# Where the persistent tiles and the second branch's tiles of a projection-bound decoder block lie in a partition

## The chip, the cores and the metric

One core of one Trainium2 chip runs the whole kernel. The metric is the device time of one execution in microseconds. An execution that the hardware profiler took gives the profile; the median of three further runs is the time that counts.

## What is computed

One hybrid decoder block on x of 512 tokens by 1024 channels, float32. A normalisation, then one wide input projection feeds two branches, whose gated outputs are merged, projected and normalised:

```python
hN = _rmsnorm(x, norm_g[l])
p = _split_in(hN @ w_in[l])            # 8992 columns, all from the same hN
mh = _mlstm(q, k, v, i_gate, f_gate)   # 4 heads x 256, q and k after a conv of width 4
ya = sigmoid(p["m_o"]) * headnorm(mh) * silu(p["m_z"])
yn = _nsa(...)                         # 8 heads x 64: compressed, selected and window attention
yb = yn * silu(p["n_z"])
merged = sigmoid(p["g_a"]) * (ya @ w_branch_a[l]) + sigmoid(p["g_b"]) * (yb @ w_branch_b[l])
x = x + merged @ w_out[l]
return _rmsnorm(x, final_norm_g)
```

With 512 tokens the selection takes every block, so the selected and the window branch are both full causal attention.

## The kernel before, in words

Every large product is done in three passes: each float32 operand is split into a high part, rounded to the matmul's input type float32r, and a low part, the residue (`split`, line 125: ACT copies the high part, DVE subtracts). hTh and hTl are the two parts of the normalised input, transposed: 128 partitions, 8 slices k of 512 tokens. Weights come in tiles of 8 slices by 128 columns (or 4 by 256): a DMA into wr, then the split into wh and wl, three buffers of each (`weights`, line 136).

A projection (`cols`, line 206) makes 128 output columns for all 512 tokens in one PSUM bank, 24 matmuls: for each of the 8 slices high weights by hTh, high weights by hTl, low weights by hTh (`passes`, line 195). The weight slice is the stationary operand, the 512 tokens are streamed:

```python
pe.matmul(ps, a, c, start=k == 0, stop=False)       # line 198: wh by hTh
pe.matmul(ps, a, d, start=False, stop=False)        # line 200: wh by hTl
pe.matmul(ps, b, c, start=False, stop=k == nk - 1)  # line 202: wl by hTh
```

The profile names a matmul by the streamed tile first, then the stationary one: pp<-hTh,wh. Each matmul also loads its stationary operand, 128 columns, which the profile lists as PEld. `passes` is a generator: the `Stream` (line 160) holds a queue of projections in a fixed order, and the other parts of the kernel take a few matmuls out of it at a time (`stream.step`, `tick`), to fill TensorE while ACT and DVE work.

The order of the work: normalisation and transposes, with a first product for small columns at line 356 (hTh and hTl are the stationary operand there); the first projections; the attention of 16 units, four projection matmuls between its steps (`tick`, line 810); then for the first branch the convolution's projections and the values, per head (`conv`, line 888, and `values`, line 909); the four heads with six matmuls between steps; then the branch stage (line 1050): for each of 8 column blocks two gate projections (`gate_ab`, streams hTh and hTl, as far as they were not done before), 24 matmuls that stream yah and yal (the first branch's output), 12 that stream ybh and ybl (the second's); last the output projection (line 1084, through `mm3`, line 152).

In the values and in the output projection the roles are turned: the weights are streamed, 256 columns wide, and 128 tokens of hTh or hTl, of meh or mel, are the stationary operand.

Where tiles lie. Each `tile` call takes the next bytes of its pool in every partition, its size rounded up to 32 bytes. The pool pers (line 91) holds, in this order, cst (5152 bytes), hTh and hTl (16384 each), mhalf, prm, cpos, rotR, gates, li, lf, ghl (2048 bytes), sel, Fc, cs and em. Without the three large ones, those behind cst sum to 32 + 352 + 128 + 512 + 384 + 64 + 64 + 32 + 64 + 64 + 64 = 1760 bytes. The pool wp follows with the nine weight buffers of 4096 bytes. Behind these lie, in the first phases, the tiles of the attention, later yah and yal, the tiles of the first branch's heads, and meh and mel. The pool ybp (line 444) is on the right side, against the upper end: ybh, ybl (8192 bytes each) and two more of 2048. gate and the compression's tiles lie below it. In the program of before the first bytes are:

| tile | first byte | modulo 512 |
|---|---|---|
| hTh, hTl | 21664, 38048 | 160 |
| wh (three buffers) | 70528, 74624, 78720 | 384 |
| wl (three buffers) | 82816, 86912, 91008 | 384 |
| yah, yal | 95104, 111488 | 384 |
| ybh, ybl | 208864, 217056 | 480 |

A slice k is 2048 bytes from the next in hTh, hTl, yah, yal, ybh and ybl, and 512 bytes (1024 where the tile is 256 columns wide) in wh and wl.

Of the kernel before, what the change touches and what calls it, by code (L numbers as in the profile page):

```python
# [12 lines left out]
F32R = mybir.dt.float32r  # L13
# [5 lines left out]
T = 512  # L19
D = 1024  # L20
NT = T // 128
ND = D // 128
# [41 lines left out]
def build(  # L64
# [26 lines left out]
    pers = ctx.enter_context(tc.tile_pool(name="pers", bufs=1))  # L91
# [13 lines left out]

    cst = pers.tile([128, CEND], F32, name="cst")
    ident = cst[:, CI : CI + 128]

    hTh = pers.tile([128, ND, T], F32R, name="hTh")
    hTl = pers.tile([128, ND, T], F32R, name="hTl")  # L110

    mhalf = pers.tile([128, 4], F32, name="mhalf")
    pool.memset(mhalf, -0.5)
# [113 lines left out]
    gates = pers.tile([128, NT, 24], F32, name="gates")  # L227
    li = pers.tile([128, NT, 4], F32, name="li")
    lf = pers.tile([128, NT, 4], F32, name="lf")
    ghl = pers.tile([128, T], F32R, name="ghl")  # L230
    sel = pers.tile([128, 4], F32R, name="sel")
    Fc = pers.tile([128, NT, 4], F32, name="Fc")
    cs = pers.tile([128, NT, 4], F32, name="cs")
    em = pers.tile([128, NT, 4], F32, name="em")

    nsa = tc.tile_pool(name="nsa", bufs=1)
    np_ = nsa.__enter__()
# [9 lines left out]
    with tc.tile_pool(name="ph0", bufs=2, side="right") as p0, tc.tile_pool(  # L247
        name="small", bufs=1, side="right"
# [194 lines left out]

    ybp = ctx.enter_context(tc.tile_pool(name="ybp", bufs=1, side="right"))
    ybh = ybp.tile([128, 4, T], F32R, name="ybh")
    ybl = ybp.tile([128, 4, T], F32R, name="ybl")
    halves = {}

    def gate_ab(base, j, pl):
# [677 lines left out]
```

## Time and profile before

| | |
|---|---|
| median of 3 runs | 649.25 us (648.68 to 649.99) |
| the profiled execution | 650.03 us |
| its span, first to last instruction | 648.2 us |
| granted TensorE clock, mean | 0.998 |

The span is what the profile covers; the 1.8 us more of the profiled execution lie around it. PE is TensorE's matmuls and PEld its loads of the stationary operand, DVE is VectorE, ACT is ScalarE, POOL is GpSimd. Ends of matmuls are modelled and matmuls overlap, so the pace of TensorE is read from the distance of starts.

### The profile page before, as it was taken

The page shows a single profiled execution, that of the slowest core. Times are in us where ns is not written, and L with a number is a line of the kernel's source. Part 1 is how long each engine was busy: PE and PEld are TensorE (multiplying, and loading weights), DVE is VectorE, ACT ScalarE, POOL GpSimd, SP SyncE. Part 2 cuts the span into 40 slices and gives each one's busy share as a digit, 9 for nine tenths or more (in the row PEclk, how much of TensorE's full clock was granted, in tenths as well). Part 3 has the DMA queues.
Part 4 walks back from the last instruction along what each step waited for, and adds up shares of the span by engine and source line. Part 5 has one row for each costly group of instructions (what it writes and reads, how often), then busy time and mean ns, then how long its engine had stood idle before and what let it go on. Part 6 is the DMA issues. An engine that isn't in the chain of part 4 may idle for free.

```text
span 648.2 us, 9274 instructions
## 1 busy us (share of the span) xinstructions
PE 632.3 (98%) x3470; PEld 538.4 (83%) x3470; DVE 412.2 (64%) x878; ACT 302.8 (47%) x604; POOL 54.0 (8%) x114
## 2 busy tenths in 40 slices
PE   6999999999999999999999999999999999999995
PEld 4988778888878788888989889888888888888995
DVE  5786777767866865557679787696554333334455
ACT  5554464655655655435545546446322322223334
POOL 5000021121121231100000000000000000000000
PEclk9999999999999999999999999999999999999999
DMA  7476411222122222223313322232274242423303
GB/s 237 121 197 162 125 54 50 61 66 66 36 64 65 64 58 72 66 74 91 97 45 86 92 71 71 61 97 67 66 247 110 68 127 66 127 69 101 95 1 129
DMA packets 90124, 58.74 MB, mean 91 GB/s; under 512 B 4016, under 2 KB 86100, under 8 KB 90080
## 3 DMA queue, kind: packets, MB, share of 16 engines
q1 hardware_dynamic: 90080, 58.16, 31.7%
q8 instruction: 27, 0.44, 0.3%
q14 instruction: 17, 0.14, 0.1%
HBM read 55.01 MB, written 2.10 MB: 88 GB/s over the span
## 4 chain that ended last, share of the span: by engine, by line
PE 90%; DVE 6%; ACT 2%; DMA 1%; issue 1%; SPq 0%; POOL 0%; DVEq 0%; POOLq 0%
PE pp L200 22%; PE pp L198 22%; PE pp L202 22%; PE pp L158 3%; PE pp L156 3%; PE pp L157 3%; PE pt L781 2%; DVE wl L80 1%; PE po L794 1%; PE ps L766 1%; PE po L793 1%; PE ps L534 1%; PE ps L767 1%; ACT wh L80 1%; DMA xt<-x 1%; PE ps L157 1%
## 5 line engine op out<-in xcount | busy, mean ns | idle before, releaser
L198 PE MATMUL pp<-hTh,wh 128*128 128x512 f32 (+1 forms) x488 | 193.7, 397 | 0.0
L200 PE MATMUL pp<-hTl,wh 128*128 128x512 f32 (+1 forms) x488 | 192.8, 395 | 0.0
L202 PE MATMUL pp<-hTh,wl 128*128 128x512 f32 (+1 forms) x488 | 192.5, 394 | 0.0
L80 DVE TENSOR_TENSOR wl<-wr,wh 128x1024 fp32r<-128x1024 f32 x88 | 109.0, 1240 | 77.0 <-ACT wh L80 76.4
L80 ACT ACTIVATE wh<-wr 128x1024 fp32r<-128x1024 f32 x88 | 92.9, 1057 | 118.1 <-PE pp L200 85.6
L202 PEld LDWEIGHTS pp<-hTh,wl 128*128 128x128 f32 x488 | 91.7, 188 | 17.9
L198 PEld LDWEIGHTS pp<-hTh,wh 128*128 128x128 f32 x488 | 91.8, 188 | 16.9
L200 PEld LDWEIGHTS pp<-hTl,wh 128*128 128x128 f32 x488 | 91.9, 188 | 16.5
L775 POOL TENSOR_SCALAR P<-P,st 128x128 f32<-128x128 f32 (+1 forms) x64 | 38.7, 625 | 182.6 <-DVE st L80 147.1
L80 ACT ACTIVATE P<-P,st 128x128 f32<-128x128 f32 (+3 forms) x64 | 35.7, 559 | 36.8 <-DVE st L80 36.7
L80 DVE CUSTOM_DVE_ANT_0 P<-ps,cst 128x128 f32<-128x128 f32 (+3 forms) x64 | 30.5, 486 | 22.3 <-PE ps L767 22.0
L80 ACT ACTIVATE pth<-pt 128x512 fp32r<-128x512 f32 (+1 forms) x64 | 27.3, 435 | 29.9 <-PE pt L781 18.7
L80 DVE TENSOR_TENSOR ptl<-pt,pth 128x512 fp32r<-128x512 f32 (+1 forms) x64 | 30.4, 485 | 16.4 <-ACT pth L80 15.8
L156 PE MATMUL pp<-wh,meh 128*128 128x256 f32 x128 | 36.2, 283 | 0.0
L157 PE MATMUL pp<-wl,meh 128*128 128x256 f32 x128 | 36.2, 283 | 0.0
L158 PE MATMUL pp<-wh,mel 128*128 128x256 f32 x128 | 36.2, 284 | 0.0
L198 PE MATMUL pp<-wh,hTh 128*128 128x256 f32 x128 | 36.0, 281 | 0.0
L202 PE MATMUL pp<-wh,hTl 128*128 128x256 f32 x128 | 35.9, 281 | 0.0
L200 PE MATMUL pp<-wl,hTh 128*128 128x256 f32 x128 | 35.9, 281 | 0.0
L80 DVE SCALAR_TENSOR_TENSOR u<-pp,prm,u 128x511 f32<-128x511 f32 (+2 forms) x48 | 35.6, 742 | 0.4
L80 DVE SCALAR_TENSOR_TENSOR s<-s,pp 128x512 f32<-128x512 f32 x16 | 11.0, 688 | 30.5 <-PE pp L202 30.5
L781 PE MATMUL pt<-cst,P 128*128 128x128 f32 x160 | 28.6, 273 | 0.3 <-DVE ptl L80 0.3
(272 smaller groups left out, 1113.0 us busy)
## 6 DMA issues: line engine op xcount, KB each, us to landing
wr<-w_in SPq DMA_DIRECT2D x68, 512.0 KB, 3.8
wr<-w_branch_a SPq DMA_DIRECT2D x8, 512.0 KB, 3.7
wr<-w_out SPq DMA_DIRECT2D x8, 512.0 KB, 3.5
wr<-w_branch_b SPq DMA_DIRECT2D x4, 512.0 KB, 3.7
xo<-x SPq DMA_DIRECT2D x1, 2048.0 KB
out<-xo SPq DMA_DIRECT2D x8, 256.0 KB, 2.2
xt<-x SPq DMA_DIRECT2D x3, 512.0 KB, 6.6
k<-k SPq DMA_DIRECT2D x8, 128.0 KB, 2.3
```

The costliest lines, as they stand in the source:

```text
L80: ins = fn(*args, **kw)
L156: pe.matmul(ps, a, c, start=start and i == 0, stop=False)
L157: pe.matmul(ps, a, d, start=False, stop=False)
L158: pe.matmul(ps, b, c, start=False, stop=stop and i == n - 1)
L198: pe.matmul(ps, a, c, start=k == 0, stop=False)
L200: pe.matmul(ps, a, d, start=False, stop=False)
L202: pe.matmul(ps, b, c, start=False, stop=k == nk - 1)
L534: pe.matmul(ph[:, :64], W1[i][:, j, :], Xs[i][:, j].rearrange("p g n -> p (g n)"), start=j == 0, stop=j == 15,)
L766: pe.matmul(pss[:, :n], tq, kh[:, b, :n], start=True, stop=False)
L767: pe.matmul(pss[:, :n], tq, kl[:, b, :n], start=False, stop=True)
L775: pool.tensor_scalar(pj, pj, st[:, 2, j : j + 1], 1.0, OP.mult, OP.mult)
L781: pe.transpose(pt[:, (qb - kb) * 128 : (qb - kb) * 128 + 128], P[:, POFF[qb] + kb * 128 : POFF[qb] + kb * 128 + 128], ident,)
```

## The change

Two declarations move and one tile grows. hTh, hTl and ghl are declared last in the pool pers, behind the small tiles; the nine weight buffers stay where they were, since the sum of sizes is the same. ybl gets 280 elements (1120 bytes) more at its end, which no instruction uses, so ybh, ybl and the pools below them on that side move down by 1120 bytes. The computation and the order of all instructions are the same.

```diff
--- before.py
+++ after.py
@@ -106,9 +106,6 @@
     cst = pers.tile([128, CEND], F32, name="cst")
     ident = cst[:, CI : CI + 128]
 
-    hTh = pers.tile([128, ND, T], F32R, name="hTh")
-    hTl = pers.tile([128, ND, T], F32R, name="hTl")
-
     mhalf = pers.tile([128, 4], F32, name="mhalf")
     pool.memset(mhalf, -0.5)
 
@@ -227,11 +224,15 @@
     gates = pers.tile([128, NT, 24], F32, name="gates")
     li = pers.tile([128, NT, 4], F32, name="li")
     lf = pers.tile([128, NT, 4], F32, name="lf")
-    ghl = pers.tile([128, T], F32R, name="ghl")
     sel = pers.tile([128, 4], F32R, name="sel")
     Fc = pers.tile([128, NT, 4], F32, name="Fc")
     cs = pers.tile([128, NT, 4], F32, name="cs")
     em = pers.tile([128, NT, 4], F32, name="em")
+
+
+    hTh = pers.tile([128, ND, T], F32R, name="hTh")
+    hTl = pers.tile([128, ND, T], F32R, name="hTl")
+    ghl = pers.tile([128, T], F32R, name="ghl")
 
     nsa = tc.tile_pool(name="nsa", bufs=1)
     np_ = nsa.__enter__()
@@ -443,7 +444,8 @@
 
     ybp = ctx.enter_context(tc.tile_pool(name="ybp", bufs=1, side="right"))
     ybh = ybp.tile([128, 4, T], F32R, name="ybh")
-    ybl = ybp.tile([128, 4, T], F32R, name="ybl")
+    ybl = ybp.tile([128, 4 * T + 280], F32R, name="ybl")[:, : 4 * T]
+    ybl = ybl.rearrange("p (c t) -> p c t", c=4)
     halves = {}
 
     def gate_ab(base, j, pl):
```

## Rows read from the trace of the kernel before

**Rows 1.** The page: busy time of each engine; the chain that ended last, by engine, by line

```profile
PE 632.3 (98%) x3470; PEld 538.4 (83%) x3470; DVE 412.2 (64%) x878; ACT 302.8 (47%) x604; POOL 54.0 (8%) x114
...
PE 90%; DVE 6%; ACT 2%; DMA 1%; issue 1%; SPq 0%; POOL 0%; DVEq 0%; POOLq 0%
PE pp L200 22%; PE pp L198 22%; PE pp L202 22%; PE pp L158 3%; PE pp L156 3%; PE pp L157 3%; PE pt L781 2%; DVE wl L80 1%; PE po L794 1%; PE ps L766 1%; PE po L793 1%; PE ps L534 1%; PE ps L767 1%; ACT wh L80 1%; DMA xt<-x 1%; PE ps L157 1%
```

**Rows 2.** Busy time by stage; columns in the first line, x counts instructions, granted clock PEclk

```profile
core 0: us, PE busy (x) PEld busy (x) DVE busy (x) ACT busy (x) POOL busy (x), PEclk, DMA share, GB/s
30.00:90.00 60.00, 58.62 (x328) 48.99 (x327) 45.20 (x131) 28.88 (x59) 2.01 (x6) 1.00 0.55 142
90.00:272.00 182.00, 180.12 (x939) 148.26 (x938) 128.79 (x316) 104.99 (x245) 36.90 (x61) 1.00 0.22 59
272.00:400.00 128.00, 128.00 (x749) 112.23 (x748) 93.93 (x168) 62.69 (x108) 2.46 (x8) 1.00 0.28 78
400.00:445.00 45.00, 45.00 (x270) 39.72 (x269) 36.10 (x69) 23.97 (x44) 1.15 (x3) 1.00 0.27 73
445.00:585.00 140.00, 140.00 (x633) 114.57 (x632) 58.74 (x86) 41.51 (x60) 1.01 (x1) 1.00 0.37 109
```

**Rows 3.** The page: costliest groups; count | busy us, mean ns | idle before, releaser

```profile
L198 PE MATMUL pp<-hTh,wh 128*128 128x512 f32 (+1 forms) x488 | 193.7, 397 | 0.0
L200 PE MATMUL pp<-hTl,wh 128*128 128x512 f32 (+1 forms) x488 | 192.8, 395 | 0.0
L202 PE MATMUL pp<-hTh,wl 128*128 128x512 f32 (+1 forms) x488 | 192.5, 394 | 0.0
L80 DVE TENSOR_TENSOR wl<-wr,wh 128x1024 fp32r<-128x1024 f32 x88 | 109.0, 1240 | 77.0 <-ACT wh L80 76.4
L80 ACT ACTIVATE wh<-wr 128x1024 fp32r<-128x1024 f32 x88 | 92.9, 1057 | 118.1 <-PE pp L200 85.6
```

**Rows 4.** Timeline of PE, branch stage: start us, us, engine, line, op, tiles, shape, count

```profile
536.96 0.39 PE L198 MATMUL pp<-hTh,wh 128*128 128x512 f32 x1
...
548.15 0.39 PE L198 MATMUL pp<-yah,wh 128*128 128x512 f32 x1
...
549.53 0.39 PE L198 MATMUL pp<-yah,wh 128*128 128x512 f32 x1
...
553.61 0.40 PE L198 MATMUL pp<-ybh,wh 128*128 128x512 f32 x1
...
556.42 0.39 PE L198 MATMUL pp<-hTh,wh 128*128 128x512 f32 x1
```

**Rows 5.** Timeline of PE: the longest run, then the values of the first head

```profile
276.36 0.45 PE L198 MATMUL pp<-hTh,wh 128*128 128x512 f32 x1
...
304.40 0.28 PE L198 MATMUL pp<-wh,hTh 128*128 128x256 f32 x1
...
315.76 0.40 PE L943 MATMUL ps<-ghl,sel 128*128 128x512 f32 x1
```

**Rows 6.** Timeline of PE: first and seventh start from the score block at line 156

```profile
316.00 0.40 PE L156 MATMUL ps<-qkh,qkh 128*128 128x512 f32 x1
...
317.40 0.40 PE L198 MATMUL pp<-hTh,wh 128*128 128x512 f32 x1
```

**Rows 7.** Timeline of PE: two starts of the output projection, 100 matmuls apart

```profile
599.94 0.28 PE L157 MATMUL pp<-wl,meh 128*128 128x256 f32 x1
...
611.94 0.28 PE L158 MATMUL pp<-wh,mel 128*128 128x256 f32 x1
```

**Rows 8.** Timeline of PE: two short runs of hTh in the attention

```profile
173.63 0.40 PE L198 MATMUL pp<-hTh,wh 128*128 128x512 f32 x1
...
174.57 0.28 PE L793 MATMUL po<-pth,vsw 128*128 128x256 f32 x1
...
178.37 0.39 PE L200 MATMUL pp<-hTl,wh 128*128 128x512 f32 x1
...
179.06 0.27 PE L781 MATMUL pt<-cst,P 128*128 128x128 f32 x1
```

## The prediction

> **What bounds the kernel now.** I read the busy times and the chain first, then the stages, then single starts on TensorE. TensorE is busy 98% of the span and 90% of the chain that ended last is its matmuls; three lines of one helper, the three passes of the projections (198, 200, 202), hold 22% each [rows 1]. By stage: from 272 to 585 us the busy time of PE equals the length of the stretch, at a granted clock of 1.00 (the 2.4 GHz level); between 90 and 272 us it lacks 1.9 us of 182 and between 30 and 90 us 1.4 us of 60 [rows 2]. So a nanosecond off the pace of a matmul is a nanosecond off the end there, and nearly so before.
>
> The engines that feed PE are ahead of it: the rounding of the weights on ACT idles 85.6 us for PE to give a buffer back, and the residue on DVE idles 76.4 us for that ACT step [rows 3]. A faster PE eats into that slack and meets nothing new.
>
> The mean duration in a group (397 ns for 512 columns [rows 3]) is not the pace, since matmuls overlap. The pace is the distance of starts. In the branch stage, one stretch after the other, it is [rows 4]:
> - 48 matmuls that stream hTh and hTl: 536.96 to 548.15, 11.19 us, **233.1 ns**;
> - 24 that stream yah and yal: the first six take 548.15 to 549.53, 230.0 ns each, the other eighteen 549.53 to 553.61, 4.08 us, **226.7 ns**;
> - 12 that stream ybh and ybl: 553.61 to 556.42, 2.81 us, **234.2 ns**.
>
> All three have the same shape (512 columns at 2.4 GHz would be 213.3 ns), the same lines, the same weight buffers, and TensorE does nothing else between them. What differs is where the streamed tile lies. The program of before puts the nine weight buffers at 384 bytes modulo 512 (wh at 70528 and 4096 bytes apart), hTh and hTl at 160 (21664, 38048), ybh and ybl at 480 (208864, 217056), yah and yal at 384 (95104, 111488), right behind the weight buffers. Slices for one k are 2048 bytes apart in the streamed tiles and 512 (1024 for the last branch) in the weights, so a pair keeps its difference for all k. Equal offsets go with 226.7 ns, 224 or 96 bytes of difference with 233 to 234 ns. I read this as the load of the next weights, which runs beside each matmul, getting in the way of the stream by an amount that depends on their relative position; after some six matmuls at equal offsets the two fall into a fixed step.
>
> **The change part by part.** It removes and adds no instruction, no DMA and no wait; each queue keeps its order. It moves tiles.
>
> *hTh and hTl.* The small persistent tiles (1760 bytes with padding, 224 modulo 512) now lie below them instead of between them and the weights, so both are at 384, like wh and wl. 1464 matmuls stream them [rows 3], 48 of these with 256 columns (the first projection, in two halves), so 1416 with 512.
> (a) Long runs from 272 us on: 120, three of 36, 30, 24, three of 12 and five of 48 matmuls, 558 in all. Their pace today: 233.1 in a run of 48 [rows 4] and 28.04 us / 120 = 233.7 ns in the longest [rows 5]; I take 233.3. At 226.7 each saves 6.6 ns: 3.68 us. Falling into step costs 6 x 3.3 = 20 ns at the start of the eight runs that follow other work: 0.16. Net **-3.52**.
> (b) Six runs of 12 to 32 between 36 and 88 us, 121 matmuls: 0.80 less 6 x 0.02, **-0.68**; PE is nearly full there, so I count it whole.
> (c) Short runs, 737 matmuls in groups of 1 to 10, mostly four between two steps of the attention. Two of them: 173.63 to 174.57, 235 ns each; behind transposes, 178.37 to 179.06, three at 230 [rows 8]. They end before a step can settle. Two rows bound what they do at equal offsets. One is the fixed step at once, 226.7: some 5.8 ns less than a middle of 232.5, -4.3 us in all. The other is the six matmuls of a score block at line 156, whose operands also both lie at 384 and which come out of other work: 316.00 to 317.40, 233.3 ns [rows 6], +0.6 us in all. The nearest row is the start of the yah stretch, 230.0 with 10 ns of rounding in 1.38 us [rows 4]; I take 231.5 rather than that, since these runs meet a different neighbour each time. 1 ns x 737: **-0.7**. In the attention part of this stage DVE is now and then the last to end, so part of it may be lost; that is inside the bounds.
>
> *Values.* 384 matmuls of 256 columns use hTh and hTl as weights and stream the weight tiles; they too become equal. Today the 96 of one head take 304.40 to 315.76, 118.3 ns each [rows 5]. The output projection has this very form at equal offsets (meh and mel at 384): 100 starts in 12.00 us, 120.0 ns [rows 7]. So here equal offsets cost: 384 x 1.7 = **+0.65**. The two fixed paces agree: 226.7 - 213.3 and 120.0 - 106.7 are both 13.3 ns, while at 224 bytes the surcharge is 20 ns for 512 columns and 11.6 for 256. Equal offsets are good for wide streams only.
>
> *ybh and ybl.* 280 elements more are 1120 bytes, 96 modulo 512; both move down from 480 to 384. 96 matmuls x (234.2 - 226.7) = **-0.72**.
>
> *yah and yal* don't move, but now follow work that is in step, so eight starts of 20 ns go: **-0.16**.
>
> *The rest.* ghl and sel feed four matmuls: nothing. The first-phase matmuls with hTh as weights (96 of 288 columns) run among waits for x; 3 ns either way is 0.3 us, in the range. gate, the compression weights and their blocks move down by 96 bytes together with their partners: no pair changes its difference. No row shows an offset that matters to ACT, DVE, POOL or a DMA; nothing.
>
> Sum: -3.52 - 0.68 - 0.7 + 0.65 - 0.72 - 0.16 = -5.1 us. The profiled execution took 650.03 us for a span of 648.2, 0.78 above the median of the runs, 649.25. So 650.03 becomes 644.9, and the median **644.1**.
>
> **A rule that speaks against it.** The rows show two paces for one shape in one stage, split by where the streamed tile lies [rows 4]. The Trainium skill, "TensorE: Matmul & The Clock Gate", section "Step-by-step: what each phase is for", says that stream and weight load have read ports of their own, so that "Loading the next tile's weights doesn't steal SBUF read bandwidth from the running matmul"; "SBUF — State Buffer", section "Who interferes with whom", says that PE waits on no one. By that rule placement could not change the pace and the sum would be 0. The trace disagrees, by 6.4 ns a matmul.
>
> **The rivals.**
> 1. *Placement is not it.* The yah stretch is faster for another reason, such as its distance from the weight buffers, and hTh at 384 goes on at 233. For: yah is also the nearest neighbour of the weights, so the trace before does not separate distance from offset. Against: ybh, far above, and hTh, below, are equally slow, and the output projection settles on the same 13.3 ns with other tiles [rows 7]. That the tiles don't get there is excluded: 160 + 224 and 480 - 96 are both 384. Time: 649.25. Chance 0.12. This is also where the rule quoted above would leave the time.
> 2. *The step spreads to the short runs.* Neighbouring score blocks lie at 384 too, so the state may survive the breaks. The same sum with (c) at its end: -5.1 - 3.6 = -8.7, 640.5. Chance 0.18. For: at 256 columns it holds through 100 matmuls of the output projection [rows 7]; against: the 233.3 ns of the score block [rows 6].
> 3. *Slower: hTh never falls into step.* If the start state, not the offset, decides, all 1416 run like the score block, which sits at equal offsets and still makes 233.3 [rows 6]: against 232.9 over long and short runs that is +0.6, and the values' +0.65 stands: +1.3, 650.5 (the ybh gain needs the step too). It decides where a run of 24 or more does not reach 227 after six matmuls. Against: yah did within seven. Chance 0.07.
>
> **How the numbers follow.** Forecast 0.63, step everywhere 0.18, nothing 0.12, slower 0.07. A measurement of this kernel can tell about 0.2%, 1.3 us, from no change. The forecast's own ends: (c) at 0 and (b) half lost, -4.1; (c) at -2.5 us, -6.9: 642.3 to 645.2. The range reaches to the spread step, 640.5, and up to a half loss of the long runs, 647.5; outside are rivals 1 and 3, 0.19. Faster 0.81, taking in the first two cases; the same 0.12; slower 0.07.
>
> **What would show it.** Right: in the branch stage hTh, yah and ybh all at 226 to 227 ns, the 120-run before the first values in 27.2 us instead of 28.04; values at 120.0 instead of 118.3, 11.52 us a head; PE still 98% busy and fewer idle microseconds on ACT. Wrong: hTh at 233 in those runs (placement was not it); the groups of four in the attention at 227 (the step spreads); new idle time on PE behind DVE wl or ACT wh (the feed was the next bound).

## The result, and the profile after

The changed kernel takes **645.37 us** (median of 6 runs, 644.98 to 646.61) against 649.43 us for the kernel before in the same session (6 runs): a ratio of 0.994 with an interval of 0.9927 to 0.9953. It is 4.1 us faster; 644.1 had been predicted, with a range of 640.5 to 647.5. Its profiled execution took 645.59 us for a span of 643.8, both 4.4 us below those of before.

The page of the changed kernel, lines that answer to [rows 1, 3]. Line numbers of the helper are three lower.

```profile
PE 627.3 (97%) x3470; PEld 538.7 (84%) x3470; DVE 411.6 (64%) x878; ACT 302.6 (47%) x604; POOL 53.6 (8%) x114
...
PE 88%; DVE 6%; ACT 2%; DMA 1%; issue 1%; SPq 0%; POOL 0%; DVEq 0%; POOLq 0%
...
L80 DVE TENSOR_TENSOR wl<-wr,wh 128x1024 fp32r<-128x1024 f32 x88 | 109.1, 1240 | 74.3 <-ACT wh L80 73.8
L80 ACT ACTIVATE wh<-wr 128x1024 fp32r<-128x1024 f32 x88 | 92.9, 1057 | 114.4 <-PE pp L197 83.0
```

TensorE is busy 627.3 us instead of 632.3, with the same 3470 instructions; the rounding of the weights on ACT and the residue on DVE take what they took, and the idle time before them went from 118.1 to 114.4 and from 77.0 to 74.3 us. Nothing else became the bound. The timeline of the branch stage answers to [rows 4]:

```profile
533.78 0.39 PE L195 MATMUL pp<-hTh,wh 128*128 128x512 f32 x1
...
544.66 0.39 PE L195 MATMUL pp<-yah,wh 128*128 128x512 f32 x1
...
550.10 0.39 PE L195 MATMUL pp<-ybh,wh 128*128 128x512 f32 x1
...
552.82 0.39 PE L195 MATMUL pp<-hTh,wh 128*128 128x512 f32 x1
```

48 matmuls of hTh in 10.88 us, 24 of yah in 5.44, 12 of ybh in 2.72: **226.7 ns** in all three, from the first to the last, where before they made 233.1, 227.7 and 234.2. The longest run and the values behind it [rows 5]:

```profile
275.56 0.45 PE L195 MATMUL pp<-hTh,wh 128*128 128x512 f32 x1
...
302.83 0.28 PE L195 MATMUL pp<-wh,hTh 128*128 128x256 f32 x1
...
314.34 0.40 PE L945 MATMUL ps<-ghl,sel 128*128 128x512 f32 x1
```

27.27 us instead of 28.04 for the 120 (227.3 ns, a longer distance behind the first matmul included), and 11.51 us instead of 11.36 for the 96 values: 119.9 ns instead of 118.3. A short run in the attention, the same one as the first of [rows 8]:

```profile
172.95 0.40 PE L195 MATMUL pp<-hTh,wh 128*128 128x512 f32 x1
...
173.88 0.28 PE L795 MATMUL po<-pth,vsw 128*128 128x256 f32 x1
```

Four in 0.93 us, 232.5 ns each against 235: no step here. Where the time went, from the distance of each matmul's start to the next in both traces (the order is the same, so they can be subtracted one by one), in us:

| stretch | change | of it |
|---|---|---|
| 0 to 36 us | -0.4 | starts and waits for x; experiments 5 and 11 differ there by 1.3 and 0.5 from the change's profile |
| 36 to 90 us | -0.1 | hTh -0.6, given back in waits, 0.35 of it in one |
| 90 to 272 us | -0.2 | hTh -0.4, others +0.2 |
| 272 to 445 us | -0.9 | hTh -1.7, values +0.6, small ones +0.2 |
| 445 to 600 us | -2.8 | hTh -1.9, ybh -0.8, yah -0.2 |
| behind 600 us | 0.0 | output projection, 120.0 ns as before |

The wait that took back most of the early gain is that of the first product of the compression, which needs its blocks from DVE. Before, then after:

```profile
48.61 0.39 PE L202 MATMUL pp<-hTh,wl 128*128 128x512 f32 x1
49.12 0.29 PE L534 MATMUL ps<-X,w1t 128*128 128x64 f32 x1
...
47.85 0.39 PE L199 MATMUL pp<-hTh,wl 128*128 128x512 f32 x1
...
48.71 0.29 PE L536 MATMUL ps<-X,w1t 128*128 128x64 f32 x1 [0.47 <-DVE Z L80]
```

TensorE now starts the last matmul ahead of it at 47.85 instead of 48.61 us, and the next start comes 0.86 us later, 0.51 before. The product itself starts 0.41 us earlier, no more than the first 36 us had given.

### The profile page after: what moved, and what is told of

It is laid out like the page before. It is cut to its first block, busy times and chain, and to the rows that moved or that the text cites. A ratio compares the mean times of both kernels' runs of the same rounds, so it can differ in the third digit from the quotient of the medians.

```text
span 643.8 us, 9274 instructions
## 1 busy us (share of the span) xinstructions
PE 627.3 (97%) x3470; PEld 538.7 (84%) x3470; DVE 411.6 (64%) x878; ACT 302.6 (47%) x604; POOL 53.6 (8%) x114
## 4 chain that ended last, share of the span: by engine, by line
PE 88%; DVE 6%; ACT 2%; DMA 1%; issue 1%; SPq 0%; POOL 0%; DVEq 0%; POOLq 0%
PE pp L197 21%; PE pp L195 21%; PE pp L199 21%; PE pp L155 3%; PE pp L153 3%; PE pp L154 3%; PE pt L783 2%; DVE wl L80 2%; PE ps L768 1%; PE po L796 1%; PE po L795 1%; PE ps L536 1%; ACT wh L80 1%; PE ps L769 1%; DMA xt<-x 1%
## 5 line engine op out<-in xcount | busy, mean ns | idle before, releaser
L80 DVE TENSOR_TENSOR wl<-wr,wh 128x1024 fp32r<-128x1024 f32 x88 | 109.1, 1240 | 74.3 <-ACT wh L80 73.8
L80 ACT ACTIVATE wh<-wr 128x1024 fp32r<-128x1024 f32 x88 | 92.9, 1057 | 114.4 <-PE pp L197 83.0
```

The source lines that it names most:

```text
L80: ins = fn(*args, **kw)
```

## The experiments

Each changed copy of the kernel ran beside the kernel before on the same chip.

**1. The offset put back, the place kept.** In the changed kernel:

```diff
-    hTh = pers.tile([128, ND, T], F32R, name="hTh")
+    hTh = pers.tile([128, ND * T + 128], F32R, name="hTh")[:, 72 : 72 + ND * T]
+    hTh = hTh.rearrange("p (k t) -> p k t", k=ND)
```

(and hTl alike)

> The changed kernel with hTh and hTl moved up by 288 bytes inside tiles that are 512 bytes longer, so they lie where the change put them (about 24 and 41 KB) but again at 160 modulo 512, while the weights, yah and ybh keep their offsets. Theory (the offset modulo 512 between the streamed tile and the weights sets the pace): hTh back to 233 ns a matmul in the branch stage, values back to 118.3, yah's first six matmuls slow again, ybh at 227; time 648.6 (645.4 plus the h, value and yah terms, -4.57 + 0.61 - 0.18 = -4.1 us, less what the waits take up). Rival (the place, not the offset): hTh stays at 227 and the time at 645.4.

Measured: 649.03 us against 649.78, a ratio of 0.9992 (0.9982 to 1.0001). Its branch stage:

```profile
535.65 0.40 PE L195 MATMUL pp<-hTh,wh 128*128 128x512 f32 x1
...
546.85 0.40 PE L195 MATMUL pp<-yah,wh 128*128 128x512 f32 x1
...
552.33 0.39 PE L195 MATMUL pp<-ybh,wh 128*128 128x512 f32 x1
...
555.05 0.40 PE L195 MATMUL pp<-hTh,wh 128*128 128x512 f32 x1
```

hTh is back at 11.20 us / 48 = 233.3 ns, yah is at 5.48 / 24 = 228.3 with its slow start, ybh stays at 2.72 / 12 = 226.7; the values are at 118.3 again. The tiles stay where the change put them but for 288 bytes, and the whole gain of hTh is lost: the offset does it, not the place. Against the kernel before, the trace keeps the 0.76 us of ybh.

**2 and 3. Each half of the change alone.** First the change without the growth of ybl:

```diff
-    ybl = ybp.tile([128, 4 * T + 280], F32R, name="ybl")[:, : 4 * T]
-    ybl = ybl.rearrange("p (c t) -> p c t", c=4)
+    ybl = ybp.tile([128, 4, T], F32R, name="ybl")
```

> The change without the growth of ybl: hTh and hTl at 384, ybh and ybl still at 480. Theory: hTh 227, yah 227 but with six slow matmuls behind hTh only where it follows ybh (not at all: hTh comes between, so yah starts in step), ybh 234 and the hTh run behind it with a slow start of 20 ns; time 645.4 + 0.76 + 0.15 = 646.3. Rival (the gain is shared by the tiles on the right side that also moved): more than 647.

Measured: 646.67 us, ratio 0.9958 (0.9945 to 0.9971).

```profile
534.42 0.40 PE L195 MATMUL pp<-hTh,wh 128*128 128x512 f32 x1
...
545.34 0.39 PE L195 MATMUL pp<-yah,wh 128*128 128x512 f32 x1
...
550.78 0.40 PE L195 MATMUL pp<-ybh,wh 128*128 128x512 f32 x1
...
553.59 0.40 PE L195 MATMUL pp<-hTh,wh 128*128 128x512 f32 x1
```

ybh takes 2.81 us as before (234.2 ns), and the 48 of hTh behind such a stretch 10.92 instead of 10.88: the slow start, 40 ns. Then the growth alone, in the kernel before:

> The kernel before with ybl grown by 280 elements alone: ybh and ybl at 384. Theory: only the 96 matmuls of the second branch gain, 227 instead of 234.6, and hold the step where yah goes before: -0.7 us, 648.7. Rival (the tiles on the right side set more than that): under 648.

Measured: 649.11 us against 649.78, ratio 0.9994 (0.9985 to 1.0003), which cannot be told from no change; in the trace the 96 matmuls are 0.76 us faster, and behind 90 us no other group differs by more than 0.1 us. The halves add up, as far as these times can tell: -3.1 and -0.7 by the medians, 3.8 in sum, and -4.1 together.

**4. The pace by itself.** A kernel that runs only the three passes, 48 matmuls for each difference:

```python
h, l = (m[:, e : e + ND * T].rearrange("p (k t) -> p k t", k=ND) for m in mv)
...
pe.matmul(ps, st[0][:, k], h[:, k], start=r + k == 0, stop=False)  # e from 0 to 124 elements
```

> Leaves out the whole block: it copies x and runs the helper's three passes by themselves, 48 matmuls for each of 32 differences between streamed tile and weights (0 to 496 bytes in steps of 16), first 512 columns streamed by 128-column weights from two 16 KB tiles, then 256 columns of weights streamed with 128 tokens as stationary operand. ACT, DVE and the DMAs stand still. Theory: at difference 0, 226.7 ns and 120.0 ns; at 288 bytes (hTh before) 233 and at 96 (ybh before) 234.6 for 512 columns; at 288 the narrow form near 118. Rival (traffic of the other engines or the distance of the tiles makes the pace): one pace for all differences.

The difference is counted as streamed less stationary first byte in the wide form (512 columns), and as stationary less streamed in the narrow form (256 columns), since each time the tile mv is the one that moves. Measured, the first start for each difference; wide form at 96, 112, then 240, 256, 272, 288 bytes; narrow form at 64 and 80, and at 256 and 272:

```profile
85.61 0.40 PE L93 MATMUL pp<-mv,st 128*128 128x512 f32 x1
...
96.80 0.39 PE L93 MATMUL pp<-mv,st 128*128 128x512 f32 x1
...
186.34 0.40 PE L93 MATMUL pp<-mv,st 128*128 128x512 f32 x1
...
197.22 0.40 PE L93 MATMUL pp<-mv,st 128*128 128x512 f32 x1
...
208.14 0.39 PE L93 MATMUL pp<-mv,st 128*128 128x512 f32 x1
...
219.26 0.40 PE L93 MATMUL pp<-mv,st 128*128 128x512 f32 x1
...
398.13 0.28 PE L105 MATMUL pp<-st,mv 128*128 128x256 f32 x1
...
403.58 0.28 PE L105 MATMUL pp<-st,mv 128*128 128x256 f32 x1
...
466.01 0.28 PE L105 MATMUL pp<-st,mv 128*128 128x256 f32 x1
...
471.76 0.28 PE L105 MATMUL pp<-st,mv 128*128 128x256 f32 x1
```

48 matmuls take 11.19 us at 96 bytes (233.1 ns), 10.88 at 240 (226.7), 10.92 at 256, 11.12 at 272; the narrow form 5.45 at 64 (113.5) and 5.75 at 256 (119.8). The settled paces, from the distances between the last 32 starts of each group, in ns (for the wide form at 0 those of the group at 256, since the first matmuls of this kernel lie 427 ns apart):

| bytes, modulo 256 | 0 | 16 | 32 | 48 | 64 | 80 | 96 | 112 | 128 | 144 | 160 | 176 | 192 | 208 | 224 | 240 |
|---|---|---|---|---|---|---|---|---|---|---|---|---|---|---|---|---|
| wide | 226.7 | 231.7 | 233.3 | 233.3 | 228.9 to 233.3 | 231.2 | 233.3 | 231.3 | 232.3 | 233.3 | 234.3 | 233.3 | 233.4 | 234.6 | 233.4 | 226.7 |
| narrow | 120.0 | 118.3 | 118.4 | 117.8 | **113.3** | 118.7 | 118.7 | 120.0 | 118.7 | 120.0 | 119.9 | 118.2 | **113.3** | 116.7 | 116.8 | 119.9 |

With ACT and the DMAs standing still, and DVE making one copy of 0.69 us at the start of each next group, the paces are those of the kernel: 233.3 at 288 (hTh before), 226.7 and 120.0 at equal offsets, 118.3 for the values before; only ybh's 234.2 at 96 bytes is 233.3 here. So the other engines have no part in it, and what counts is the difference modulo 256 bytes, not 512: each difference above 255 bytes has the pace of the one 256 below (but for 64 and 320 in the wide form, 233.3 and 228.9, of which experiment 9 tells more). In every wide run of these experiments it is the streamed tile that moves and the weights that keep their offset, so for this form they don't separate the difference from the streamed tile's own address modulo 256; for the narrow form either tile was moved, the stationary one here and the streamed one in experiments 7 and 10, with the same paces.

The Trainium skill says on "TensorE: Matmul & The Clock Gate", "Step-by-step: what each phase is for", that loading the next weights doesn't take read bandwidth from the running matmul. The one pace for every place that the prediction drew from it is not what the sweep shows: the same matmuls settle at 226.7 to 234.6 ns by their addresses alone. Whether it is the load that costs this, no run here shows.

**5. Half a row further.** Experiment 1 with 64 elements in the place of 72.

> The changed kernel with hTh and hTl 256 bytes further in their rows: 128 modulo 512, against 384 of the weights. From the sweep, where 0 and 256, and 240 and 496, had the same pace: 226.7 ns in long runs, values at 120, time that of the change, 645.4. If only equality modulo 512 counts: hTh at 233, 649.

Measured: 646.95 us in one execution, whose first 36 us were 1.3 longer than in the change's profile (waits for x); behind them no group of matmuls differs from the change by more than 0.15 us, and hTh has 226.7 in its long runs, values 119.9. Equal offsets modulo 512 are thus more than is needed: equal modulo 256 does.

**6. Sixteen bytes short.** As experiment 1 with 60 elements and 64 of padding.

> The changed kernel with hTh and hTl 16 bytes short of the weights' offset (240 modulo 256). In the sweep this difference was at 226.7 ns from the second matmul on, while 0 and 256 took six to eight. If the slow starts at 0 are what the short runs lack, hTh in the attention comes from 231.5 to about 228, with long runs at 226.7 and values at 120.0: 737 x 3/4 x 4 ns = 2.2 us, of which DVE may keep half in the attention: 643.2 to 644.3. If the other neighbours of a short run set its pace: 645.4.

Measured: 648.63 us, ratio 0.9987 (0.9978 to 0.9995): the gain is gone, and no expectation held. The trace has three paces for one difference: the run of 120, a run of 36, a run of 48.

```profile
276.02 0.44 PE L195 MATMUL pp<-hTh,wh 128*128 128x512 f32 x1
...
304.46 0.28 PE L195 MATMUL pp<-wh,hTh 128*128 128x256 f32 x1
...
333.17 0.39 PE L195 MATMUL pp<-hTh,wh 128*128 128x512 f32 x1
...
341.34 0.27 PE L1008 MATMUL pt<-cst,num 128*128 128x128 f32 x1
...
497.08 0.40 PE L195 MATMUL pp<-hTh,wh 128*128 128x512 f32 x1
...
508.29 0.39 PE L195 MATMUL pp<-yah,wh 128*128 128x512 f32 x1
```

28.44 us / 120 = 237.0 ns, 8.17 / 36 = 226.9, 11.21 / 48 = 233.5. The runs of 36 come out of the heads' products, the long one out of the attention, those of 48 out of ybh. The sweep, which slid from one difference into the next, had seen only the fast one.

**7 and 8. The narrow form with its weights 64 bytes in.** The buffers of wh and wl get 64 elements more, and the weights of the 256-column blocks start o elements in (16 in the values and in the output projection). The stationary tile then lies 64 bytes before the streamed one, which is 192 in the count of experiment 4:

```diff
-        hi = wp.tile([128, nk, n], F32R, name="wh", tag="wh", bufs=3)
+        hi = wp.tile([128, nk * n + 64], F32R, name="wh", tag="wh", bufs=3)[:, o : o + nk * n]
...
-        stream.add(lambda: wwide(wv, MV + h * 256), gen)
+        stream.add(lambda: wwide(wv, MV + h * 256, 16), gen)
...
-            wh, wl = wwide(wov, cc * 256)
+            wh, wl = wwide(wov, cc * 256, 16)
```

> The changed kernel with the 256-column weight tiles of the values and the output projection 64 bytes into their buffers (each buffer 256 bytes longer), so that the stationary tile lies 64 bytes before the streamed one. In the sweep the narrow form made 113.3 ns there (192 modulo 256) and 120.0 at equal offsets: 768 matmuls x 6.7 ns = 5.1 us, 640.3, if TensorE is still the last there; the output projection's DVE and ACT are busy half the time, so little should be kept. Rival (the sweep's pace needs idle engines beside it): less than 2 us.

Measured: **642.36 us**, ratio 0.9887 (0.9872 to 0.9902), 3.0 us under the change; 5.1 had been expected. Values, and the output projection before and behind its early stop:

```profile
303.33 0.28 PE L196 MATMUL pp<-wh,hTh 128*128 128x256 f32 x1
...
314.64 0.40 PE L946 MATMUL ps<-ghl,sel 128*128 128x512 f32 x1
...
590.67 0.28 PE L154 MATMUL pp<-wh,meh 128*128 128x256 f32 x1
...
593.03 0.28 PE L156 MATMUL pp<-wh,mel 128*128 128x256 f32 x1
...
597.81 0.28 PE L154 MATMUL pp<-wh,meh 128*128 128x256 f32 x1
...
603.48 0.28 PE L156 MATMUL pp<-wh,mel 128*128 128x256 f32 x1
```

The values make 11.31 us / 96 = 117.8 ns, and so do the first matmuls of the output projection (20 in 2.36 us). Behind two waits near 593.8 us it settles at 113.3, and keeps that to the end: 50 in 5.67 us. Again two paces for one difference, where the sweep had shown 113.3 alone. The next kernel joined this with experiment 6 (60 elements for hTh and hTl, weights 12 elements in for the values, 16 for the output projection):

> Both: hTh and hTl at 240, the values' weight tiles 48 bytes in, the output projection's 64 bytes in, all other operands as in the change. If the two add up: 645.4 - 5.1 - 1 to 2 = 638.2 to 639.3.

Measured: 647.63 us, ratio 0.9965 (0.9954 to 0.9976). hTh has the paces of experiment 6, the values 118.3, and the output projection stays at 118.0 on average, since its stop, of the same length, this time left it at 117.8. (The eleven executions lie in two groups, four at 646.0 to 646.4 us and seven at 647.3 to 648.5, with the profiled one among these; an output projection at 113.3 would be 1.8 us shorter, so a stop that leaves now one pace, now the other would do it. No trace of the quicker group is there to show it.)

**9. Six entries.** The sweep's kernel with each difference entered six ways:

```python
entries = [
    lambda: wide(bank("en", 3), 0, 12), lambda: wide(bank("en", 3), 24, 12),
    lambda: narrow(bank("en", 3), 0, 12), lambda: short(bank("en", 3), 8),
]  # then twice behind a stop: the only bank of its tag waits for its copy
```

> Leaves out the whole block, as the sweep did. For 16 differences from 0 to 240 bytes the same stretch (36 matmuls of 256 columns, then 24 of 512) is entered in six ways: behind 12 wide matmuls at difference 0, 12 wide at 96, 12 narrow at 0, 8 of 128 columns, and twice behind a stop for the bank's evacuation. Theory of memory (a difference can have two settled paces, and what ran before decides): at 240 wide some entries at 226.7 and others near 236, as the changed kernel with 240 ran; at 192 narrow some at 113.3 and others at 117.8; at 0 one pace alone, 226.7 and 120.0, whatever the entry. Rival (the full kernels differ from the sweep for another reason, the buffers' places or the other engines): one pace per difference, 226.7 at 240 and 113.3 at 192, for all entries.

Measured, ns over the last twelve distances, seven of the 32 rows. The fifth group found its bank free, so it follows the fourth of its own difference without a stop, and goes on in its pace. The sixth has a stop ahead of it (0.9 us from start to start) in the wide form at 240 alone; in every other row three wide matmuls at 0, which belong to the next entry, ran just ahead of it, and some 0.1 us is lost behind its first matmul:

| | behind wide at 0 | wide at 96 | narrow at 0 | 128 columns | behind itself | sixth group |
|---|---|---|---|---|---|---|
| wide, 0 | 226.7 | 226.7 | 226.7 | 226.7 | 226.7 | 226.7 |
| wide, 64 | 228.9 | 228.9 | 233.3 | 228.8 | 228.9 | 228.9 |
| wide, 240 | 233.3 | 226.7 | 236.7 | 236.7 | 236.7 | 233.3 |
| narrow, 0 | 120.0 | 120.0 | 120.0 | 120.0 | 120.0 | 120.0 |
| narrow, 64 | 117.8 | 113.3 | 117.8 | 113.3 | 113.3 | 113.3 |
| narrow, 192 | 117.8 | 117.8 | 113.3 | 117.8 | 117.8 | 117.8 |
| narrow, 224 | 116.7 | 116.7 | 116.7 | 117.8 | 117.8 | 116.7 |

From the timeline (equal neighbours merged: start, time, count): the narrow form at 64 bytes behind the first two entries, then the wide form at 240 behind the first three, with the second and third entry between:

```profile
155.15 4.40 PE L103 MATMUL pp<-st,mv 128*128 128x256 f32 x36
...
162.18 4.25 PE L103 MATMUL pp<-st,mv 128*128 128x256 f32 x36
...
1178.62 5.76 PE L95 MATMUL pp<-mv,st 128*128 128x512 f32 x24
1184.22 2.98 PE L95 MATMUL en<-mv,st 128*128 128x512 f32 x12
1187.03 5.61 PE L95 MATMUL pp<-mv,st 128*128 128x512 f32 x24
1192.48 1.59 PE L103 MATMUL en<-st,mv 128*128 128x256 f32 x12
1193.90 5.84 PE L95 MATMUL pp<-mv,st 128*128 128x512 f32 x24
```

36 narrow matmuls take 4.40 or 4.25 us, 24 wide ones 5.76, 5.61 or 5.84. Some differences have two or three settled paces, and what ran before decides among them. (The bank of the sums alone does not: of three in rotation, the first and the fourth group of a difference have the same one, and wide at 240 and narrow at 64 differ between them.) Of the two that matter here, 0 has one only, whatever the entry, which fits that the change works in every long run and the 16-byte neighbour did not. The table does not foretell every stretch of the kernel: at 192 it has 113.3 behind narrow matmuls alone, and experiment 7 reached that behind a stop.

**10 and 11. Each narrow block by its entry, beside the change.** Experiment 7 with 8 elements for the values and 48 for the output projection, 224 and 64 bytes in the count of experiment 4; and the change once more.

> The changed kernel with each narrow block at the difference that its own entry settles best at, by the run with six entries: the values come out of wide matmuls in step, where 224 bytes (weights 32 bytes in) settles at 116.7 and both 64 and 192 at 117.8; the output projection comes out of the same and then of a stop, where 64 bytes (weights 192 bytes in) settles at 113.3. Theory of memory: values 116.7, 384 x 3.3 = -1.3 us against the change, output projection 117.8 until its early stop and 113.3 behind it, -2.4 us: 641.7, and 0.4 us under the version with 192 everywhere. Rival (the kernel's entries are not the sweep's): values at 117.8 or more, no better than 642.4.

> The changed kernel once more beside it on the same chip: 645.4, with the same paces as before (226.7 in long runs, 231.5 in the attention, values 119.9), and so 3.5 us behind the other.

Measured: 642.65 us, ratio 0.9893 (0.9878 to 0.9908), and 645.61, ratio 0.9946 (0.9925 to 0.9967), against 649.77. The 96 values:

```profile
302.59 0.28 PE L196 MATMUL pp<-wh,hTh 128*128 128x256 f32 x1
...
313.79 0.39 PE L946 MATMUL ps<-ghl,sel 128*128 128x512 f32 x1
```

11.20 us, 116.7 ns as the table has it behind wide matmuls in step. The output projection is at 113.3 behind its stop. In the trace the values are 0.4 us faster than in experiment 7; the medians of the two versions, from two sets of runs, can't be told apart, so the theory of memory has its paces here, but not its 641.7 us. Both beat the kernel before by 1.1% and the change by 0.5%.

## Why the prediction was right

The mechanism held as it was put: the streamed tile's offset against the weights' sets the pace. Term by term, predicted and measured in us:

| step | predicted | measured |
|---|---|---|
| (a) long runs of hTh from 272 us on | -3.5 | -3.6, with some -0.25 of the heads' short runs in it |
| (b) long runs before 90 us | -0.7 | -0.1: matmuls -0.6, waits +0.4, of which 0.35 at one |
| (c) short runs | -0.7 | -0.2 in the attention's stage, -0.25 in the heads (counted in a) |
| values | +0.65 | +0.61 |
| ybh | -0.72 | -0.76 |
| yah | -0.16 | -0.18 |
| before 36 us | 0 | -0.4, no effect of the change that can be named |

The step that was mis-sized is (b): I counted it whole because PE was "nearly full there", and the waits behind the missing 1.4 us of that stretch [rows 2], one above all, swallowed it. A stretch at 98% can still hold a time at which an operand arrives that TensorE doesn't set, and what is won ahead of it is lost. (c) was near in its sum, -0.45 of -0.7, but not made up as I thought. The attention's runs went from 232.4 to 231.6 ns (means of the distances under 260 ns), 0.4 us in all, and the stage got only 0.2 us shorter: the streams of 256 and 384 columns between them slowed by 0.1 us, and waits of others grew by 0.1. The heads' runs of six stayed at 231.8, and their runs of ten were in step from the first matmul, as was the score block ahead of them. The change doesn't move its operands, and its 233.3 ns at equal offsets [rows 6] had served as one of the two bounds:

```profile
314.57 0.39 PE L153 MATMUL ps<-qkh,qkh 128*128 128x512 f32 x1
...
315.93 0.39 PE L195 MATMUL pp<-hTh,wh 128*128 128x512 f32 x1
```

Six in 1.36 us are 226.7 ns each: equal offsets were not enough for the block before; what it gained came with the values ahead of it, which now lie at equal offsets too.

The top of the range, 647.5, was not what it was said to be: with half of the long runs' 3.5 us lost the sum is -3.4, 645.9; 647.5 takes the loss of every other gain besides. The measured time lies under both.

The first rival (the place) fell with experiment 1. The second (the step spreads to the short runs) came in full for the heads' runs of ten alone, 0.25 us; those of four and six did not reach it. The third (hTh never falls into step) did not come either, but two of the three kinds of runs in experiment 6 do this at another offset: its price, some 3 us above the change, shows that the rival was real, but difference 0 has one settled pace only. The outcome that was drawn from the Trainium skill's rule, no change, did not come.

The inner cause is open. That the load of the next weights meets the stream fits all of this (the surcharge over 512 or 256 columns at 2.4 GHz is 13.3 ns at difference 0 in both widths, and 6.7 in the best narrow state), but no run took the load away from the matmul, so it was argued and not shown. Nor is it shown for 512 columns that the difference counts and not the streamed tile's own address, since the weights never moved there.

## What to carry to other kernels

Before counting on a pace of TensorE, take the distance of starts in a long run and compare stretches of the same shape whose tiles lie differently: here 226.7 against 233 ns came from addresses alone, and 113.3 against 120 from addresses and, at one and the same difference, from what ran before. Put the streamed tile of a 512-column matmul at the weights' offset modulo 256 bytes; for 256 columns try a stationary tile 64 or 192 bytes past the streamed one. And try it in the kernel, since a sweep shows one settled pace where there may be three.

## What the runs showed that was not expected

- The difference counts modulo 256 bytes, not 512: 32 differences in steps of 16 bytes gave the same paces twice over in both widths, but for 64 and 320 at 512 columns.
- A settled pace depends on what ran before: at 240 bytes 226.7, 233.3 or 236.7 ns for 512 columns, at 64 and 192 bytes 113.3 or 117.8 for 256, and it then holds over runs of 120 (237.0) and of more than 300 matmuls (113.3).
- The best pace for 512 columns and the best for 256 lie at different differences (0, and 64 or 192), so a tile that is streamed in one place and stationary in another, as hTh is, can't have both without a second offset of the weights.
- One execution of the changed kernel, the profiled one of experiment 11, took 649.55 us while the other five were at 645.0 to 646.2. Its line of granted clocks has one low slice, at 49 to 65 us:

```profile
PEclk9997999999999999999999999999999999999999
```

The matmuls of 64 columns there took 1.2 us longer and those of hTh 2.0, eight of them at 427 ns from start to start: the 1.2 GHz level. A single profile may carry such a thing, and it is as large as the effect that is sought.
